# Seven-product form of the up-projection: ScalarE's copy of the first product's first half goes ahead of the last three activations of the pair done last

## The chip, the cores and the metric

One core of a Trainium2 chip runs the whole kernel. The metric is device time in microseconds (us), the median of several executions. The five engines that the text names work in parallel, each through its own queue in order: PE (TensorE), DVE (VectorE), ACT (ScalarE), POOL (GpSimd) and SP (SyncE, which here only issues DMAs). ACT issues DMAs too, from the same queue as its arithmetic.

## The reference

A decoder block over 1024 tokens of width 1024 in float32: two token mixers, then a gated feed-forward part with a causal convolution of width 3. The change lies in the feed-forward part alone:

```
def conv_ffn(h, w_up, conv_w, conv_b, w_down):
    u = h @ w_up                                   # 1024 x 5632
    up = jnp.pad(u, ((0, 0), (CONV_WIDTH - 1, 0), (0, 0)))
    u = sum(up[:, i:i + T] * conv_w[i] for i in range(CONV_WIDTH)) + conv_b
    gate, val = jnp.split(u, 2, axis=-1)           # 22 tiles of 128 columns each
    return (jax.nn.gelu(gate, approximate=True) * val) @ w_down
```

## The kernel before, in words

Every float32 operand is split into a high part (`w_hi`, cast on ACT) and a low part (`w_lo`, a subtraction on POOL or DVE), and a product is three matmuls per block of 128 rows: high by high, high by low, low by high (helper `mm3`, lines 224 to 226).

The up-projection goes over 22 pairs of column tiles (one gate tile j, one value tile j + 22), for two halves of the tokens (`hf` 0 and 1, 512 each). Pairs 3 to 21 (`n` = 0 to 18 in the loop) use a seven-product form: sums and differences of weight blocks and of token blocks replace the eight half products by seven, each of 12 matmuls into one PSUM bank. In the order of the code they are: pX from `w1` (first half), pZ from `w2`, pT from `w2`, pY from `w3`, pX again (second half, added to the same bank), pZ from `w3`, pT from `w4`. The text calls them X1, Z1, T1, Y, X2, Z2 and T2. For the first four pairs (`n` under `NEAR`) X1 and X2 were made earlier and come from DRAM, so the rest speaks of `n` = 4 to 18.

Between the products stand steps that empty the banks: ACT copies X1 to `s1` (line 1188) and Z1 to `s5` (line 1193); DVE adds T1 to `s5` (line 1195) and Y to `s1` (line 1197); ACT copies X2 to `ub` (line 1200); POOL adds `s1` and `s5` (line 1201); DVE adds Z2 and T2 to `s1` (lines 1203 and 1205). X2 is added to the bank that the copy at line 1188 reads, so it waits for that copy; T2 is added to the bank that line 1195 reads.

Then come, for two halves by two tiles, the convolution (`conv`: an activation on ACT at line 1065, two DVE operations at 1066 and 1068) and the gate (`gate`: a Gelu on ACT at 1073, a DVE product at 1074, and the DMA of the result to DRAM, `f_d`, issued from ACT at 1075).

The weights of the next pairs are prepared beside this: SP loads them to `st1` and `st2`, DVE forms `sa` (lines 1168 and 1169), `st2` (1171) and `st1` (1172), ACT casts each and POOL or DVE subtracts (`cut`, lines 1164 and 1165). `sa` has one buffer only: DVE may write the `sa` of the next pair when POOL's subtraction from the present one is over.

The order of each queue is set by the scheduler of the kernel's language, which takes what is ready in a modelled time line, with the order of the code and given priorities behind it: the preparation of weights has `high_priority(offset=WPRIO)`. After the last pair the down-projection follows: it loads `f_d` again (`f_st`, cast to `f_hl` at line 1241, subtraction at 1242) and its weights (lines 212 and 218).

Of the kernel before, what the change touches and what calls it, by code (L numbers as in the profile page):

```python
# [12 lines left out]
AF = mybir.ActivationFunctionType  # L13
# [15 lines left out]
E05 = math.exp(-0.5)  # L29
TWO_PI = 2.0 * math.pi  # L30
WPRIO = 500
MAGIC = 12582912.0
C1 = 6.25
C2 = 0.033203125
# [124 lines left out]
def body(tc, nc, xT, xN, pos, wch, wbrw, wbret, wout, wup, wdn, w2a2, gw2, rows, vecs, consts0, consts1, out):  # L159
    V, S, G, PE = nc.vector, nc.scalar, nc.gpsimd, nc.tensor  # L160
    ctx = ExitStack()

    @contextmanager
    def tile_pool(**kw):
        with tc.tile_pool(**kw) as pool:
            yield Lines(pool)

    with ctx:
# [14 lines left out]
        def C(name):  # L183
            t, o, n = COFF[name]
            return cst[t][:, o:o + n]

        def VC(name):
            o, n = VOFF[name]
            return vct[:, o:o + n]
# [5 lines left out]
        def bank(name, tag="A"):  # L195
            return psB.tile([128, 512], F32, tag=tag, name=name, bufs=BANKS[tag])
# [5 lines left out]
        def load_w(src, kt, full=None, hi=None, lo=None, st=None, eng=None):  # L202

            wp, nb = wpools[cnt[0] % len(wpools)]
            with tc.high_priority(offset=WPRIO if cnt[0] > 3 else 0):
                if st is None:
                    st = wp.tile([128, full or kt, 128], F32, tag="ws", name="w_st", bufs=nb[0])[:, 0:kt, :]
                nc.sync.dma_start(st, src)
            with tc.high_priority(offset=WPRIO if cnt[0] > 1 else 0):
                if hi is None:  # L210
# [64 lines left out]
        with tile_pool(name="x0", bufs=2, reuse_waits="tile") as xp:  # L275
# [22 lines left out]
            for q in range(NJ):  # L298
                xn = xp.tile([128, D], F32, tag="xn", name="xn", bufs=3)
                nc.sync.dma_start(xn, xN[128 * q:128 * q + 128, :])  # L300
                S.activation(xn, xn, AF.Square, accum_out=rsm[:, q:q + 1])
            with tc.high_priority(offset=WPRIO):
                V.tensor_scalar(rsm[:, 8:16], rsm[:, 0:8], 1.0 / D, RMS_EPS, ALU.mult, ALU.add)
# [10 lines left out]
        def proj(w, ps, hf, ts=slice(0, 512)):  # L314
            hi, lo = w
            mm3(ps[:, ts], [(hi[:, k, :], lo[:, k, :], hn[k][hf][0][:, ts], hn[k][hf][1][:, ts]) for k in range(KT)])
# [11 lines left out]
        with pctx, tile_pool(name="p1", bufs=1, reuse_waits="tile", side="right") as p1:  # L328
# [160 lines left out]
            V.tensor_scalar(n, ang, 1.0 / TWO_PI, C("turn"), ALU.mult, ALU.add)  # L489
            V.tensor_scalar(n, n, MAGIC, MAGIC, ALU.add, ALU.subtract)  # L490
            for c_ in (C1, C2, C3):
# [14 lines left out]
        def qk_pair(m):  # L506

            ws = [load_w(wch[14 + 2 * m + e], 8) for e in range(2)]
            for hf in range(2):
                h_ = slice(hf * 512, (hf + 1) * 512)  # L510
                ab = []
                for e in range(2):
                    ps = psA.tile([128, 512], F32, tag="a", name="ps_side")
                    proj(ws[e], ps, hf)
                    with tc.high_priority(offset=WPRIO):
                        t = gp.tile([128, 512], F32, tag=f"qk{e}", name="qk", bufs=1)
# [17 lines left out]
        def side_tile(i):  # L534

            w = load_w(wch[i], 8)
            for hf in range(2):
                ps = psA.tile([128, 512], F32, tag="a", name="ps_side")
                proj(w, ps, hf)
                with tc.high_priority(offset=WPRIO):  # L540
                    ot = gp.tile([128, 512], F32, tag="ot", name="ot")
# [237 lines left out]
        def first_stage(j):  # L779

            nonlocal R
            tk = slice(j * 128, (j + 1) * 128)
            with tc.high_priority(offset=WPRIO):
                zvg = t2.tile([128, 24, 128], F32, name="zvg")
# [272 lines left out]
        def mmb(ps, w, ks, B, first, last):  # L1057
            mm3(ps, [(w[0][:, k, :], w[1][:, k, :], B[n][0], B[n][1]) for n, k in enumerate(ks)],
                first=first, last=last, skip=not first)

        def conv(pool, ub, b, j, src):

            i = j + FT * b
            u = pool.tile([128, 512], F32, tag=f"u{b}", name="u_f")
            S.activation(u, src, AF.Identity, bias=VC("cb")[:, i:i + 1], scale=VC("cw2")[:, i:i + 1])  # L1065
            V.scalar_tensor_tensor(out=u, in0=ub[:, 1:513], scalar=VC("cw1")[:, i:i + 1], in1=u,  # L1066
                                   op0=ALU.mult, op1=ALU.add)
            V.scalar_tensor_tensor(out=u, in0=ub[:, 0:512], scalar=VC("cw0")[:, i:i + 1], in1=u,  # L1068
                                   op0=ALU.mult, op1=ALU.add)
            return u  # L1070

        def gate(j, hf, u0, u1):
            S.activation(u0, u0, AF.Gelu_apprx_tanh)
            V.tensor_tensor(out=u0, in0=u0, in1=u1, op=ALU.mult)
            nc.scalar.dma_start(f_d[hf, j], u0)

# [66 lines left out]
        fp = fctx.enter_context(tile_pool(name="fp", bufs=2, reuse_waits="tile"))  # L1143
        W8 = [128, 8, 128]
        lh, rh_ = slice(0, 4), slice(4, 8)

        for n, j in enumerate(range(NSTD, FT)):
            with tc.high_priority(offset=WPRIO):
                st1 = wp.tile(W8, F32, tag="ws", name="w_st", bufs=2)
                nc.sync.dma_start(st1, wup[j])  # L1150

                st2 = wx.tile(W8, F32, tag="ws", name="w_st", bufs=2) if n else w3s.tile(W8, F32, tag="ws", name="w_st")
                nc.sync.dma_start(st2, wup[j + FT])
                sa = wx.tile(W8, F32, tag="sa", name="w_sa") if n else w3s.tile(W8, F32, tag="wh", name="w_sa")
                if n >= NEAR:
                    w1 = wp.tile(W8, F32R, tag="wh", name="w_hi", bufs=3), wx.tile(W8, F32R, tag="wl", name="w_lo", bufs=3)
                wh = (wx, 2) if n else (wp, 3)
                w2 = (wh[0].tile(W8, F32R, tag="wh", name="w_hi", bufs=wh[1]),
                      wx.tile(W8, F32R, tag="wl", name="w_lo", bufs=3) if n else w3s.tile(W8, F32R, tag="wl", name="w_lo"))
                w3 = wp.tile(W8, F32R, tag="wh", name="w_hi", bufs=3), wp.tile(W8, F32R, tag="wl", name="w_lo", bufs=2)  # L1160
                w4 = wh[0].tile(W8, F32R, tag="wh", name="w_hi", bufs=wh[1]), wp.tile(W8, F32R, tag="wl", name="w_lo", bufs=2)

                def cut(w, ks, src, eng):
                    S.copy(w[0][:, ks, :], src)  # L1164
                    eng.tensor_tensor(out=w[1][:, ks, :], in0=src, in1=w[0][:, ks, :], op=ALU.subtract)  # L1165
                if n >= NEAR:
                    cut(w1, slice(0, 8), st1, G)
                V.tensor_tensor(out=sa[:, lh, :], in0=st2[:, lh, :], in1=st2[:, rh_, :], op=ALU.add)  # L1168
                V.tensor_tensor(out=sa[:, rh_, :], in0=st1[:, lh, :], in1=st2[:, lh, :], op=ALU.subtract)  # L1169
                cut(w2, slice(0, 8), sa, G)  # L1170
                V.tensor_tensor(out=st2[:, lh, :], in0=sa[:, lh, :], in1=st1[:, lh, :], op=ALU.subtract)
                V.tensor_tensor(out=st1[:, rh_, :], in0=st1[:, rh_, :], in1=st2[:, lh, :], op=ALU.subtract)
                cut(w3, lh, st2[:, lh, :], G)
                cut(w3, rh_, st1[:, rh_, :], G)
                cut(w4, lh, st2[:, rh_, :], V)
            if n >= NEAR:
                pX = psA.tile([128, 512], F32, tag="a", name="ps_x")
            pZ = bank("ps_z", "B")
            pT = bank("ps_t", "CY"[n % 2])
            pY = bank("ps_y", "AI"[n % 2])  # L1180
            ub = [fp.tile([128, 1026], F32, tag=f"ub{b}", name="ub") for b in range(2)]
            for b in range(2):
                G.memset(ub[b][:, 0:2], 0.0)
            s1 = fp.tile([128, 512], F32, name="s1")
            s5 = fp.tile([128, 512], F32, name="s5")
            if n >= NEAR:
                mmb(pX, w1, range(4), hn2[0][0:4], True, True)
                S.copy(s1, pX)
            else:
                nc.sync.dma_start(s1, e_d[n, 0])  # L1190
                nc.sync.dma_start(ub[0][:, 2:514], e_d[n, 1])
            mmb(pZ, w2, range(4), T1, True, True)
            S.copy(s5, pZ)
            mmb(pT, w2, range(4, 8), T3, True, True)
            V.tensor_tensor(out=s5, in0=pT, in1=s5, op=ALU.add)
            mmb(pY, w3, range(4), T2, True, True)
            V.tensor_tensor(out=s1, in0=pY, in1=s1, op=ALU.add)
            if n >= NEAR:
                mmb(pX, w1, range(4, 8), hn2[0][4:8], False, True)
                S.copy(ub[0][:, 2:514], pX)  # L1200
            G.tensor_tensor(out=ub[1][:, 514:1026], in0=s1, in1=s5, op=ALU.add)
            mmb(pZ, w3, range(4, 8), hn2[1][4:8], False, True)
            V.tensor_tensor(out=ub[0][:, 514:1026], in0=pZ, in1=s1, op=ALU.add)  # L1203
            mmb(pT, w4, range(4), T4, False, True)
            V.tensor_tensor(out=ub[1][:, 2:514], in0=pT, in1=s1, op=ALU.add)
            for hf in range(2):
                cv = [conv(fp, ub[b][:, 512 * hf:512 * hf + 514], b, j, ub[b][:, 512 * hf + 2:512 * hf + 514])
                      for b in range(2)]
                gate(j, hf, *cv)
        fctx.close()  # L1210
        w3ctx.close()

# [103 lines left out]
```

## Time and profile before

| what | us |
|---|---|
| median of 3 runs (1887.44 to 1890.42) | 1888.04 |
| the profiled execution, its own time | 1895.04 |
| its span, first to last instruction | 1893.2 |
| PE busy in the span | 1786.2 |
| DVE busy | 1182.6 |
| ACT busy | 649.9 |
| POOL busy | 687.0 |

The profiled execution is 7.00 us longer than the median of the runs. PE is busy in 94% of the span, but a busy PE is not PE at its peak, since the ends of matmuls are modelled; what counts is where PE stands still, and behind whom. The seven-product pairs with X1 and X2 (`n` = 4 to 18) fill about 1300 to 1618 us of the span.

### The profile page before, as it was taken

What the parts mean: (1) busy time and instruction counts of PE and PEld (TensorE: products, weight loads), DVE (VectorE), ACT (ScalarE), POOL (GpSimd) and SP (SyncE); (2) the same over time, 40 slices, a digit from 0 to 9 for tenths busy, and PEclk for the clock granted to TensorE, in tenths of its full rate; (3) what the DMA queues carried; (4) which work ended last, traced back from release to release, by engine and by line L of the source; (5) the groups of instructions that cost most, each with busy time, mean ns of one, the idle gap of its engine ahead of it and who ended that gap; (6) DMA issues with size and microseconds to landing.
All of it is one profiled execution on the core that took longest, in us unless ns stands there. A gap on an engine that the chain in (4) does not pass through costs nothing.

```text
span 1893.2 us, 27391 instructions
## 1 busy us (share of the span) xinstructions
PE 1786.2 (94%) x10610; PEld 1448.0 (76%) x10610; DVE 1182.6 (62%) x2068; ACT 649.9 (34%) x993; POOL 687.0 (36%) x491
## 2 busy tenths in 40 slices
PE   8779999999999999999999999888999999989996
PEld 7667778788777788888788778676777777868885
DVE  4786584755666634663444837789888887753413
ACT  6543211111111113322343435544434444443320
POOL 1344523311122122111463744554554454222523
PEclk9989999999999999999999999999999999999998
DMA  8233532433423225555653835433222222665531
GB/s 287 86 114 100 186 86 70 134 90 89 115 88 115 72 84 159 176 178 167 205 167 102 261 116 168 167 117 99 85 78 72 86 69 88 218 205 144 188 92 45
DMA packets 202690, 244.44 MB, mean 129 GB/s; under 512 B 60992, under 2 KB 136256, under 8 KB 201536
## 3 DMA queue, kind: packets, MB, share of 16 engines
q1 hardware_dynamic: 125712, 171.11, 29.8%
q10 hardware_dynamic: 76848, 71.59, 11.6%
q8 instruction: 83, 1.36, 0.3%
q14 instruction: 47, 0.39, 0.1%
HBM read 177.10 MB, written 65.54 MB: 128 GB/s over the span
## 4 chain that ended last, share of the span: by engine, by line
PE 53%; DVE 18%; DMA 8%; issue 4%; POOL 3%; ACT 3%; ACTq 0%; SPq 0%; DVEq 0%; POOLq 0%
PE ps_side L225 7%; PE ps_side L224 7%; PE ps_side L226 7%; DVE u_f L1066 4%; PE ps_dn L226 3%; PE ps_dn L225 3%; PE ps_dn L224 3%; DMA w_st<-in_wup_dram 2%; DVE u_f L1068 2%; POOL w_lo L1165 2%; DVE w_sa L1169 2%; PE ps_o L225 1%; PE ps_o L226 1%; PE ps_o L224 1%; DVE w_sa L1168 1%
## 5 line engine op out<-in xcount | busy, mean ns | idle before, releaser
L218 POOL TENSOR_TENSOR w_lo<-w_st,w_hi 128x1024 fp32r<-128x1024 f32 (+2 forms) x111 | 259.8, 2341 | 515.7 <-ACT w_hi L212 183.5
L212 ACT CAST w_hi<-w_st 128x1024 fp32r<-128x1024 f32 (+2 forms) x162 | 161.7, 999 | 412.6 <-PE ps_side L225 130.7
L225 PE MATMUL ps_side<-hnl,w_hi 128*128 128x512 f32 x640 | 256.2, 400 | 0.0
L224 PE MATMUL ps_side<-hnh,w_hi 128*128 128x512 f32 x640 | 255.6, 399 | 0.0
L226 PE MATMUL ps_side<-hnh,w_lo 128*128 128x512 f32 x640 | 254.9, 398 | 0.0
L224 PEld LDWEIGHTS ps_side<-hnh,w_hi 128*128 128x128 f32 x640 | 121.0, 189 | 26.9 <-issue 1.5
L225 PEld LDWEIGHTS ps_side<-hnl,w_hi 128*128 128x128 f32 x640 | 121.0, 189 | 26.5 <-issue 1.5
L226 PEld LDWEIGHTS ps_side<-hnh,w_lo 128*128 128x128 f32 x640 | 121.1, 189 | 26.3 <-issue 0.8
L218 DVE TENSOR_TENSOR w_lo<-w_st,w_hi 128x1024 fp32r<-128x1024 f32 (+1 forms) x51 | 65.2, 1279 | 82.3 <-ACT w_hi L212 40.6
L1066 DVE SCALAR_TENSOR_TENSOR u_f<-ub,vct,u_f 128x512 f32<-128x512 f32 x88 | 102.1, 1164 | 13.2 <-ACT u_f L1065 11.5
L1165 POOL TENSOR_TENSOR w_lo<-w_st,w_hi 128x512 fp32r<-128x512 f32 (+1 forms) x53 | 105.5, 2012 | 3.8 <-ACT w_hi L1164 2.3
L1065 ACT ACTIVATE u_f<-ub,vct 128x512 f32<-128x512 f32 x76 | 59.8, 812 | 124.4 <-DVE ub L1203 99.2
L224 PE MATMUL ps_rw<-hnh,w_hi 128*128 128x512 f32 (+1 forms) x224 | 87.7, 392 | 13.1 <-ACT hnh L289 6.8
L225 PE MATMUL ps_rw<-hnl,w_hi 128*128 128x512 f32 (+1 forms) x224 | 86.7, 387 | 0.5 <-DVE hnl L290 0.5
L226 PE MATMUL ps_rw<-hnh,w_lo 128*128 128x512 f32 (+1 forms) x208 | 80.0, 385 | 0.0
L226 PE MATMUL ps_b<-y_hi,w_lo 128*128 128x512 f32 x192 | 75.2, 392 | 2.8 <-DVE w_lo L218 1.8
L1068 DVE SCALAR_TENSOR_TENSOR u_f<-ub,vct,u_f 128x512 f32<-128x512 f32 x88 | 76.9, 892 | 0.2
L224 PE MATMUL ps_b<-y_hi,w_hi 128*128 128x512 f32 x192 | 75.2, 392 | 0.7 <-ACT w_hi L212 0.6
L225 PE MATMUL ps_b<-y_lo,w_hi 128*128 128x512 f32 x192 | 74.9, 390 | 0.0
L224 PE MATMUL ps_dn<-f_k,w_hi 128*128 128x512 f32 (+1 forms) x198 | 72.4, 366 | 0.0
L226 PE MATMUL ps_dn<-f_k,w_lo 128*128 128x512 f32 (+1 forms) x198 | 72.4, 366 | 0.0
L225 PE MATMUL ps_dn<-f_k,w_hi 128*128 128x512 f32 (+1 forms) x198 | 72.2, 366 | 0.0
(418 smaller groups left out, 4346.6 us busy)
## 6 DMA issues: line engine op xcount, KB each, us to landing
w_st<-in_wup_dram SPq DMA_DIRECT2D x54, 512.0 KB, 3.5
w_st<-in_wch_dram SPq DMA_DIRECT2D x52, 512.0 KB, 3.9
w_st<-in_wdn_dram SPq DMA_DIRECT2D x38, 512.0 KB, 4.0
pj_d<-ot ACTq DMA_DIRECT2D x64, 256.0 KB, 2.2
zvg<-pj_d SPq DMA_DIRECT2D x8, 1536.0 KB, 8.9
f_d<-u_f ACTq DMA_DIRECT2D x44, 256.0 KB, 2.1
L<-L_d SPq DMA_DIRECT2D x8, 1344.0 KB, 5.9
w_st<-in_wbret_dram SPq DMA_DIRECT2D x16, 512.0 KB, 3.9
```

The source lines that it names most:

```text
L212: S.copy(hi, st)
L218: eng.tensor_tensor(out=lo, in0=st, in1=hi, op=ALU.subtract)
L224: PE.matmul(ps, wh, xh, start=first and a == 0, stop=False, skip_group_check=skip)
L225: PE.matmul(ps, wh, xl, start=False, stop=False, skip_group_check=skip)
L226: PE.matmul(ps, wl, xh, start=False, stop=last and a == n - 1, skip_group_check=skip)
L1065: S.activation(u, src, AF.Identity, bias=VC("cb")[:, i:i + 1], scale=VC("cw2")[:, i:i + 1])
L1066: V.scalar_tensor_tensor(out=u, in0=ub[:, 1:513], scalar=VC("cw1")[:, i:i + 1], in1=u, op0=ALU.mult, op1=ALU.add)
L1068: V.scalar_tensor_tensor(out=u, in0=ub[:, 0:512], scalar=VC("cw0")[:, i:i + 1], in1=u, op0=ALU.mult, op1=ALU.add)
L1165: eng.tensor_tensor(out=w[1][:, ks, :], in0=src, in1=w[0][:, ks, :], op=ALU.subtract)
L1168: V.tensor_tensor(out=sa[:, lh, :], in0=st2[:, lh, :], in1=st2[:, rh_, :], op=ALU.add)
L1169: V.tensor_tensor(out=sa[:, rh_, :], in0=st1[:, lh, :], in1=st2[:, lh, :], op=ALU.subtract)
```

## The change

The last part of a pair's work (the two value halves' convolution, the second Gelu, the gate products and their DMAs) is put into a function `rest`, which the next pair calls just behind its copy of X1, at priority offset `GPRIO` and with an ordering edge: what `rest` puts on ACT's queue stands behind that copy. The gate halves' convolutions and the first Gelu stay where they were.

```
+GPRIO = 40
...
-        def gate(j, hf, u0, u1):
-            S.activation(u0, u0, AF.Gelu_apprx_tanh)
+        def gate(j, hf, u0, u1, gelu=True):
+            if gelu:
+                S.activation(u0, u0, AF.Gelu_apprx_tanh)
...
             if n >= NEAR:
                 mmb(pX, w1, range(4), hn2[0][0:4], True, True)
-                S.copy(s1, pX)
+                c1 = S.copy(s1, pX)
+                with tc.issue_after(c1.ins), tc.high_priority(offset=GPRIO):
+                    rest()
             else:
+                rest()
...
-            for hf in range(2):
-                cv = [conv(fp, ub[b][:, 512 * hf:512 * hf + 514], b, j, ub[b][:, 512 * hf + 2:512 * hf + 514])
-                      for b in range(2)]
-                gate(j, hf, *cv)
+            def part(b, hf, j=j, ub=ub):
+                return conv(fp, ub[b][:, 512 * hf:512 * hf + 514], b, j, ub[b][:, 512 * hf + 2:512 * hf + 514])
+
+            u0 = [part(0, hf) for hf in range(2)]
+            S.activation(u0[0], u0[0], AF.Gelu_apprx_tanh)
+
+            def rest(j=j, part=part, u0=u0):
+                gate(j, 0, u0[0], part(1, 0), gelu=False)
+                gate(j, 1, u0[1], part(1, 1))
+        rest()
```

The queues of PE, POOL and SP keep their order. ACT's and DVE's change at the same places in 14 pairs. ACT's queue before, in a pair in the middle (s1_13051 is the copy of X1; u_f the convolution's result; w_sa the sum of weights that is cast for the next pair; f_d the result in DRAM):

```order
L1164 CAST w_hi_13027<-w_st_13018 128x512
L1065 ACTIVATE u_f_12998<-ub_12897,vct_76 128x512
L1065 ACTIVATE u_f_13009<-ub_12897,vct_76 128x512
L1073 ACTIVATE u_f_13005<-u_f_13005 128x512
L1188 COPY s1_13051<-ps_x_13043 128x512
L1193 COPY s5_13052<-ps_z_13044 128x512
L1075 DMA f_d_10242<-u_f_12994 128x512
L1075 DMA f_d_10242<-u_f_13005 128x512
L1164 CAST w_hi_13174<-w_sa_13171 128x1024
```

ACT's queue now, the same place (s1_13038 is the copy; lines are those of the changed file, up to 17 higher):

```order
L1169 CAST w_hi_13014<-w_st_13005 128x512
L1195 COPY s1_13038<-ps_x_13030 128x512
L1066 ACTIVATE u_f_13053<-ub_12884,vct_76 128x512
L1066 ACTIVATE u_f_13059<-ub_12884,vct_76 128x512
L1075 ACTIVATE u_f_12998<-u_f_12998 128x512
L1203 COPY s5_13039<-ps_z_13031 128x512
L1077 DMA f_d_10242<-u_f_12994 128x512
L1169 CAST w_hi_13161<-w_sa_13158 128x1024
L1077 DMA f_d_10242<-u_f_12998 128x512
```

The copy has gone ahead of three activations, and, besides, the cast of w_sa has gone ahead of the second DMA to f_d. This second exchange stands in 13 of the 14 pairs; in the last it is the cast of an f_hl that goes ahead of the DMA.

On DVE one operation of the convolution changes places with the difference at line 1172; before and now, in another pair:

```order
L1165 TENSOR_TENSOR w_lo_12877<-w_st_12867,w_hi_12876 128x512
L1066 SCALAR_TENSOR_TENSOR u_f_12847<-ub_12746,vct_76,u_f_12847 128x512
L1172 TENSOR_TENSOR w_st_13016<-w_st_13016,w_st_13018 128x512
L1066 SCALAR_TENSOR_TENSOR u_f_12858<-ub_12746,vct_76,u_f_12858 128x512
L1068 SCALAR_TENSOR_TENSOR u_f_12847<-ub_12746,vct_76,u_f_12847 128x512
```

and on DVE now:

```order
L1170 TENSOR_TENSOR w_lo_12864<-w_st_12854,w_hi_12863 128x512
L1177 TENSOR_TENSOR w_st_13003<-w_st_13003,w_st_13005 128x512
L1067 SCALAR_TENSOR_TENSOR u_f_12902<-ub_12733,vct_76,u_f_12902 128x512
L1067 SCALAR_TENSOR_TENSOR u_f_12908<-ub_12733,vct_76,u_f_12908 128x512
L1069 SCALAR_TENSOR_TENSOR u_f_12902<-ub_12733,vct_76,u_f_12902 128x512
```

The difference of weights comes one place sooner and the value half's first operation one place later; all else stays. In the last pair, where the down-projection's work mixes in, an f_hl cast on ACT goes ahead of the activations too, and its subtraction on DVE ahead of four convolution operations. ACT's queue there before:

```order
L1164 CAST w_hi_13631<-w_st_13622 128x512
L1065 ACTIVATE u_f_13602<-ub_13501,vct_76 128x512
L1065 ACTIVATE u_f_13613<-ub_13501,vct_76 128x512
L1073 ACTIVATE u_f_13609<-u_f_13609 128x512
L1241 CAST f_hl_13797<-f_st_13795 128x512
L1188 COPY s1_13655<-ps_x_13647 128x512
```

There the cast stood last but one. ACT's queue at the same place now (s1_13642 is the copy):

```order
L1169 CAST w_hi_13618<-w_st_13609 128x512
L1258 CAST f_hl_13797<-f_st_13795 128x512
L1195 COPY s1_13642<-ps_x_13634 128x512
L1066 ACTIVATE u_f_13657<-ub_13488,vct_76 128x512
L1066 ACTIVATE u_f_13663<-ub_13488,vct_76 128x512
L1075 ACTIVATE u_f_13602<-u_f_13602 128x512
```

Here the copy stands behind a cast that waits for a load from DRAM, as it did before, and both stand ahead of the activations.

## Rows read from the trace of the kernel before

**Rows 1.** Waits by engine, 1340 to 1590 us: total us, times, longest

```profile
ACT w_hi L1164 <- DVE u_f L1074: 37.4, 12, 3.3
DVE w_sa L1168 <- POOL w_lo L1165: 33.6, 12, 2.9
...
PE ps_x L224 <- ACT s L1188: 15.3, 13, 1.3
```

**Rows 2.** Timeline of PE, 1440 to 1465: start, duration, [idle before, releaser]

```profile
1444.58 0.39 PE L226 MATMUL ps_y<-b_hi,w_lo 128*128 128x512 f32 x1
1446.13 0.50 PE L224 MATMUL ps_x<-b_hi,w_hi 128*128 128x512 f32 x1 [1.16 <-ACT s L1188]
...
1451.72 0.39 PE L224 MATMUL ps_t<-b_hi,w_hi 128*128 128x512 f32 x1
...
1454.44 0.39 PE L224 MATMUL ps_x<-b_hi,w_hi 128*128 128x512 f32 x1
```

**Rows 3.** Timeline of ACT, 1440 to 1465

```profile
1442.57 0.61 ACT L1164 CAST w_hi<-w_st 128x512 fp32r<-128x512 f32 x1
1443.57 1.52 ACT L1065 ACTIVATE u_f<-ub,vct 128x512 f32<-128x512 f32 x2 [0.39 <-DVE ub L1205]
1444.99 0.61 ACT L1073 ACTIVATE u_f<-u_f 128x512 f32<-128x512 f32 x1
1445.51 0.56 ACT L1188 COPY s<-ps_x 128x512 f32<-128x512 f32 x1
1445.98 0.58 ACT L1193 COPY s<-ps_z 128x512 f32<-128x512 f32 x1
1448.68 0.93 ACTq L1075 DMA_DIRECT2D f_d<-u_f  x2
1449.65 1.05 ACT L1164 CAST w_hi<-w_sa 128x1024 fp32r<-128x1024 f32 x1 [3.09 <-DVE u_f L1074]
```

**Rows 4.** Timeline of DVE, 1440 to 1465

```profile
1442.85 0.68 DVE L1205 TENSOR_TENSOR ub<-ps_t,s 128x512 f32<-128x512 f32 x1
...
1447.96 1.29 DVE L1074 TENSOR_TENSOR u_f<-u_f 128x512 f32<-128x512 f32 x2
1449.16 0.69 DVE L1195 TENSOR_TENSOR s<-ps_t,s 128x512 f32<-128x512 f32 x1
1449.76 0.68 DVE L1197 TENSOR_TENSOR s<-ps_y,s 128x512 f32<-128x512 f32 x1
1453.21 1.77 DVE L1168 TENSOR_TENSOR w_sa<-w_st 128x512 f32<-128x512 f32 x1 [2.77 <-POOL w_lo L1165]
```

**Rows 5.** Timeline of POOL, 1440 to 1465

```profile
1450.78 2.40 POOL L1165 TENSOR_TENSOR w_lo<-w_sa,w_hi 128x1024 fp32r<-128x1024 f32 x1 [2.52 <-ACT w_hi L1164]
1453.14 1.29 POOL L1201 TENSOR_TENSOR ub<-s,s 128x512 f32<-128x512 f32 x1
```

**Rows 6.** Chain that ended last: start, us, what

```profile
1350.58 1.77 DVE w_sa L1168
...
1449.28 0.33 ACTq L1075
...
1576.39 1.77 DVE w_sa L1168
```

**Rows 7.** Timeline, 1326 to 1337: a POOL pass beside DVE

```profile
1327.35 2.62 POOL L1165 TENSOR_TENSOR w_lo<-w_sa,w_hi 128x1024 fp32r<-128x1024 f32 x1
...
1327.63 0.69 DVE L1195 TENSOR_TENSOR s<-ps_t,s 128x512 f32<-128x512 f32 x1
...
1328.23 2.29 DVE L1074 TENSOR_TENSOR u_f<-u_f 128x512 f32<-128x512 f32 x1
```

**Rows 8.** Timeline of ACT, 1585 to 1640, the last pair

```profile
1608.61 0.60 ACT L1241 CAST f_hl<-f_st 128x512 fp32r<-128x512 f32 x1
...
1614.08 0.62 ACT L1241 CAST f_hl<-f_st 128x512 fp32r<-128x512 f32 x1 [3.91 <-DMA f_st<-f_d]
```

**Rows 9.** Waits of PE, 1590 to 1700

```profile
PE ps_dn L226 <- DVE w_lo L218: 5.8, 4, 2.8
```

More of the change, by code (lines that the diff above doesn't have):

```diff
@@ L1145, in body, with rest @@
         lh, rh_ = slice(0, 4), slice(4, 8)
+        def rest():
+            pass
         for n, j in enumerate(range(NSTD, FT)):
```

## Prediction

> **What bounds the kernel now.** I read the page's slices first, then the waits of the stretch of regular pairs, the chain that ended last, and the timelines of PE, ACT, DVE and POOL in one pair. In the waits the reader sees one entry for PE that matters: the second half of the first product (X2) waits for ACT's copy of the first half, 13 times in this window [rows 1]. On PE's timeline, Y's last matmul starts at 1444.58 and X2's first at 1446.13 [rows 2]; undisturbed matmuls follow each other by a twelfth of a product, and a product takes 2.72 us (1451.72 to 1454.44, [rows 2]), so 0.23 us. X2 could have started at 1444.81 and is 1.32 us late. ACT's timeline says why: the copy at 1445.51 stands behind two activations and a Gelu that start at 1443.57 and 1444.99 [rows 3], though X1, which it reads, was done long before: the next pair's X1 starts at 1454.44 [rows 2], so this pair's, one period of 20.53 us (below) earlier, at 1433.9, and it was over at 1436.6.
>
> But PE's wait isn't what sets the period. The chain passes line 1168 at 1350.58 and at 1576.39 [rows 6], 11 periods later: (1576.39 - 1350.58) / 11 = 20.53 us a pair. PE needs 7 x 2.72 = 19.04. In the chain between there is no PE. It goes round like this: DVE's two gate products (1447.96, 1.29 us, [rows 4]), ACT's two DMA issues of their results (from 1448.68, [rows 3]; the second at 1449.28, [rows 6]), ACT's cast of `sa` (1449.65, after 3.09 us of idling, [rows 3]), POOL's subtraction from it (1450.78, after 2.52 us of idling, [rows 5]), DVE's next write of the one `sa` buffer (1453.21, after 2.77 us of idling, [rows 4]), and through DVE's queue back to the gate products. Three engines stand idle in turn there, each released by the one before: 37.4 us for ACT and 33.6 us for DVE in 12 pairs [rows 1]. PE runs beside this ring and loses in each pair what the ring is longer.
>
> **The copy, moved ahead.** It would follow the cast at 1442.57, 0.61 us long [rows 3]. ACT idles 0.39 us there before the two activations, which wait for DVE's line 1205 (1442.85 + 0.68 = 1443.53, [rows 4]). The copy occupies ACT for 0.47 us (1445.51 to the next start, 1445.98, [rows 3]). Starting about 1443.1, it ends its turn about 1443.57, when the activations started anyway: hidden, or 0.1 us late at the most. DVE takes their first result one place later than before, so that 0.1 is covered too. The price of the move is nothing; were that idle time gone, it would be 0.47 us a pair.
>
> What it gives: X2 no longer waits and PE gains 1.32 us once. It then meets the next wait on the same ring. T2 must not start before DVE's line 1195 has read its bank, at 1449.16 + 0.69 = 1449.85 [rows 4]. With X2 at 1444.81, T2 comes 2 x 2.72 us later, at 1450.25: 0.40 us to spare. In the next pairs PE gains again and waits at T2 instead of X2. So alone this move is worth 1.32 + 0.40 = 1.7 us once, not once per pair.
>
> **The cast of `sa`, moved ahead of the second DMA issue.** This is a side effect of the new order, and it is on the ring. The cast follows the last issue's start by 1449.65 - 1449.28 = 0.37 us. Behind the first issue, at 1448.68, it starts at 1449.05: 0.60 us sooner. Its data and buffer are ready then: `sa` was written in DVE's pass before the gate products, and the bank of weights it overwrites belonged to T1, which PE left before Y, done by 1444.8. POOL's subtraction, DVE's write of `sa`, and all behind them come 0.60 us sooner, and the next pair starts that much sooner: a period of 19.93 us, still above PE's 19.04. The second DMA issue now comes while the cast runs; its landing frees a buffer that is written again only in the next pair's convolution, and the down-projection reads the result far later. 13 casts of `sa` are moved so: 13 x 0.60 = 7.8 us.
>
> Bounds of this term: below, what POOL's pass costs if it overlaps DVE. A pass beside DVE took 2.62 us [rows 7], one by itself 2.40 [rows 5]: 0.22 us, so 0.38 us a pair, 4.9 in all. Above, all that the ring is longer than PE: 20.53 - 19.04 = 1.49 us a pair, 13 x 1.49 = 19.4. I take 0.60, since the nearest rows give it directly, and DVE's lines 1195 and 1197, which POOL's earlier pass would meet, ran at their full speed beside such a pass (0.69 us, [rows 7]).
>
> **DVE's exchange** of a weights difference with a convolution operation: same operations, same sum, no POOL pass beside either (POOL is idle from the end of its previous passes to 1450.78 but for two small fills, [rows 5] shows 2.52 us of idling at its end). Nothing; at most 0.1 us either way.
>
> **The end of the stretch.** In the last pair a cast of `f_hl` (1608.61) comes ahead of the activations, and its subtraction goes ahead of four DVE operations of about 0.7 us. The load of the next `f_st` waits for that subtraction, and ACT later idled 3.91 us for such a load [rows 8]. So between 0 and 4 x 0.7 = 2.8 us sooner. PE's lead of 1.7 us arrives here as well. But the down-projection's start is itself held by its weights (5.8 us of PE waits, [rows 9]), which come by the same DVE, ACT and DMA queues: PE's lead is mostly waited away. Of both together, 0 to 4.5 us, I take 0.7, near the lower end because of that row.
>
> **Sum.** 7.8 + 0.7 = 8.5 us from the profiled execution's 1895.04: 1886.5. That execution is 7.0 us above the median of the runs, so the median goes from 1888.04 to 1879.5.
>
> **A rule weighed.** In rows 7 DVE's gate product beside POOL's pass took 2.29 us, line 1195 beside the same pass 0.69. The Trainium skill, "SBUF — State Buffer", section "Who interferes with whom", says that DVE and GpSimd share a port pair as an exclusive lock, and that it is taken by DVE operations with two SBUF inputs, not by those with one. By that rule lines 1195 and 1197 (one input from PSUM) never wait for POOL, and the earlier pass is free; without it the loss of the fourth case below would be open. The trace agrees in that one pass.
>
> **Rivals.**
> 1. *The ring doesn't shorten, PE's wait only moves from X2 to T2.* For it: DVE, ACT and POOL pass the work round with other waits close by, and one that this trace hides behind the first could step in. Against it: each step of the ring shows idle time of over 2.5 us before it, so nothing else is near. What remains is PE's lead: 1888.04 - 1.7 = 1886.3, less than can be told from no change.
> 2. *The ring loosens altogether and PE's work becomes the bound.* For it: DVE's 1.77 us at line 1168 is mostly POOL's 1.29 us beside it [rows 4, 5], and a small shift can let DVE go first; then several alternating passes shorten. Against it: POOL's next pass starts as its previous one ends, ahead of DVE in the same way as now. Time: 1888.04 - 19.4 = 1868.6.
> 3. *Partial:* the ring gives back 0.2 to 0.4 us of each 0.6. That lies inside the forecast's own range below.
> 4. *Slower.* POOL's pass starts before line 1197 and holds it, as it held the gate product in rows 7. It decides if the pass comes 1450.78 - 1449.76 = 1.02 us sooner relative to DVE; I expect 0.60, so 0.42 us are missing. Then: POOL from 1450.18 to 1452.80, line 1197 until 1453.40, POOL's sum of `s1` and `s5`, which needs it, until 1454.69 (1.29 us, [rows 5]), line 1168 until 1455.29. Now it ends at 1453.21 + 1.77 = 1454.98 [rows 4]. That is 0.31 us a pair later, 13 x 0.31 = 4.0: 1892.0.
>
> **How the numbers follow.** Forecast with its partial case 0.68, rival 1 0.19, rival 2 0.08, rival 4 0.05. About 0.2%, 3.8 us, is what a measurement of this kernel can tell from no change. The forecast's own range goes from 1876 (7.8 + 4.5 saved) to 1884 (4.9 less what the end can cost); nearly all of it is faster by over 0.2%, and so is rival 2. Rival 1 is no change; rival 4 is slower. So faster 0.74, same 0.20, slower 0.06. The range reaches down to 1873, more than halfway to rival 2, and up to 1888 to take in rival 1.
>
> **What would show it.** In the changed kernel's chain, line 1168's successor should come every 19.9 us, not 20.5. ACT's idle time before the cast of `sa` should fall from 3.09 to about 2.5 us, with a DMA issue on either side of it. PE's wait for the copy at X2 should be gone, and a wait for line 1195 at T2 of about 0.9 us a pair should stand in its place. A period still at 20.5 with a T2 wait of 1.5 us is rival 1; PE without waits is rival 2; a DVE line 1197 of over 2 us is rival 4. A gain that shows at 1590 us and is gone at 1700 would mean that the down-projection's loads waited it away, and my term for the end is wrong.

## The result and the profile after

The changed kernel takes 1880.38 us (median of 6 runs, 1876.79 to 1884.47), the kernel before 1889.23 us in the runs beside it (1887.40 to 1895.29): a ratio of 0.9945, 95% interval 0.9928 to 0.9962, and 8.85 us less by the medians (by the ratio it would be 10.4, with 7.2 to 13.6 as its interval). The profiled execution took 1881.99 us with a span of 1880.2.

The chain that ended last still goes through DVE's write of `sa`, now line 1173 (start, us, what; to be set beside [rows 6]):

```profile
1349.22 1.76 DVE w_sa L1173
...
1446.22 2.41 POOL w_lo L1170
1448.65 1.77 DVE w_sa L1173
...
1568.00 1.76 DVE w_sa L1173
```

11 pairs lie between the first and the last row: (1568.00 - 1349.22) / 11 = 19.89 us a pair, where the kernel before took 20.53. The same engines follow each other; the way round has become 0.64 us shorter.

The waits of the changed kernel, 1340 to 1590 us, against [rows 1]:

```profile
ACT w_hi L1169 <- DVE u_f L1076: 38.3, 13, 3.0
DVE w_sa L1173 <- POOL w_lo L1170: 26.0, 12, 2.2
...
PEld ps_t L225 <- DVE s L1205: 10.4, 12, 0.9
PE ps_t L225 <- DVE s L1205: 5.4, 12, 0.5
...
PEld ps_x L225 <- ACT s L1195: 2.3, 11, 0.2
```

In this window PE no longer waits for ACT's copy at the second half of the first product; its weight loads (PEld) do for 0.2 us. A wait for DVE's line 1205 has come at the second half of the third. The waits of ACT and DVE for each other's work are still there, only shorter: they are the ring.

One pair of the changed kernel on ACT (against [rows 3]), by the timeline from 1438 us:

```profile
1438.62 0.60 ACT L1169 CAST w_hi<-w_st 128x512 fp32r<-128x512 f32 x1
1439.12 0.57 ACT L1195 COPY s<-ps_x 128x512 f32<-128x512 f32 x1
1439.61 1.52 ACT L1066 ACTIVATE u_f<-ub,vct 128x512 f32<-128x512 f32 x2
1441.04 0.62 ACT L1075 ACTIVATE u_f<-u_f 128x512 f32<-128x512 f32 x1
1441.56 0.56 ACT L1203 COPY s<-ps_z 128x512 f32<-128x512 f32 x1
1444.73 0.33 ACTq L1077 DMA_DIRECT2D f_d<-u_f  x1
1445.09 1.05 ACT L1169 CAST w_hi<-w_sa 128x1024 fp32r<-128x1024 f32 x1 [2.97 <-DVE u_f L1076]
1445.33 0.33 ACTq L1077 DMA_DIRECT2D f_d<-u_f  x1
```

The copy takes the place of the idle 0.39 us ahead of the activations, which are not late: 1439.61 - 1438.62 = 0.99 us behind the cast's start, 1.00 before. The cast of `sa` now lies between the two DMA issues, 0.36 us behind the first one's start.

The same pair on DVE (against [rows 4]):

```profile
1444.01 1.29 DVE L1076 TENSOR_TENSOR u_f<-u_f 128x512 f32<-128x512 f32 x2
1445.21 0.69 DVE L1205 TENSOR_TENSOR s<-ps_t,s 128x512 f32<-128x512 f32 x1
1445.81 0.68 DVE L1207 TENSOR_TENSOR s<-ps_y,s 128x512 f32<-128x512 f32 x1
1448.65 1.77 DVE L1173 TENSOR_TENSOR w_sa<-w_st 128x512 f32<-128x512 f32 x1 [2.15 <-POOL w_lo L1170]
```

Line 1173 starts 1448.65 - 1444.01 = 4.64 us behind the gate products' start, and 1453.21 - 1447.96 = 5.25 before: 0.61 us less. POOL, by its timeline (against [rows 5]), brings it that far:

```profile
1446.22 2.40 POOL L1170 TENSOR_TENSOR w_lo<-w_sa,w_hi 128x1024 fp32r<-128x1024 f32 x1 [1.91 <-ACT w_hi L1169]
```

In the last pair PE does wait for the copy at X2: there the copy stands behind the cast of `f_hl`, which starts only after 1.43 us of idling (ACT, then PE):

```profile
1598.80 0.62 ACT L1258 CAST f_hl<-f_st 128x512 fp32r<-128x512 f32 x1 [1.43 <-issue]
1599.33 0.58 ACT L1195 COPY s<-ps_x 128x512 f32<-128x512 f32 x1
```

```profile
1599.96 0.50 PE L225 MATMUL ps_x<-b_hi,w_hi 128*128 128x512 f32 x1 [0.89 <-ACT s L1195]
```

### The profile page after: what moved, and what is told of

The parts are those of the page before. It is cut to its first block, busy times and chain, and to the rows that moved or that the text cites. A ratio compares the mean times of both kernels' runs of the same rounds, so it can differ in the third digit from the quotient of the medians.

```text
span 1880.2 us, 27392 instructions
## 1 busy us (share of the span) xinstructions
PE 1788.0 (95%) x10610; PEld 1448.4 (77%) x10610; DVE 1182.3 (63%) x2068; ACT 648.3 (34%) x993; POOL 686.6 (37%) x491
## 4 chain that ended last, share of the span: by engine, by line
PE 56%; DVE 18%; DMA 5%; issue 4%; POOL 3%; ACT 3%; ACTq 0%; SPq 0%; DVEq 0%; POOLq 0%
PE ps_side L226 7%; PE ps_side L225 7%; PE ps_side L227 7%; DVE u_f L1067 4%; PE ps_dn L227 4%; PE ps_dn L226 4%; PE ps_dn L225 4%; DVE u_f L1069 2%; POOL w_lo L1170 2%; PE ps_o L226 1%; PE ps_o L227 1%; PE ps_o L225 1%; DVE w_sa L1174 1%; DVE w_sa L1173 1%; PE ps_b L227 1%
```

## The experiments

All were timed in 5 rounds beside the kernel before; e1 to e4 on one chip, e6 and e7 on another. A period that covers the whole stretch is read from one row of ACT's grouped timeline, 1290 to 1650 us (start of the first and the last of the 15 casts of `sa`; 14 pairs lie between). It is the distance of the casts; where PE's own work becomes the bound, the distance of PE's products has to be read beside it (e3, e6). The three kernels in which it decides most, before, e2 and e1:

```profile
L1164 ACT CAST w_hi<-w_sa x15: 1039/1052/1059, 1306.0 to 1593.3; 128x1024 fp32r<-128x1024 f32 x15
```

```profile
L1171 ACT CAST w_hi<-w_sa x15: 1032/1048/1057, 1300.3 to 1587.9; 128x1024 fp32r<-128x1024 f32 x15
```

```profile
L1166 ACT CAST w_hi<-w_sa x15: 1040/1054/1057, 1307.6 to 1586.7; 128x1024 fp32r<-128x1024 f32 x15
```

That is 287.3 us before, 287.6 in e2 and 279.1 in e1; the changed kernel has 279.0 (1305.3 to 1584.3).

**e1, the cast alone.** The kernel before, and the second DMA issue put behind the cast of `sa`; on no other engine does the order change.

```diff
-            nc.scalar.dma_start(f_d[hf, j], u0)
+            fdma.append(nc.scalar.dma_start(f_d[hf, j], u0))
...
-                    S.copy(w[0][:, ks, :], src)
+                    c = S.copy(w[0][:, ks, :], src)
+                    if src is sa and n > NEAR + 1:
+                        tc.add_manual_dep(fdma[-3].ins, c.ins.name, ...)
```

> The kernel before with one half of the change alone: on ACT the cast of sa goes ahead of the second of the two DMA issues of the gate products, in 13 pairs; the copy of s1 stays behind the activations. Ring theory (the period is set by gate products, DMA issues, cast, POOL's subtraction, DVE's write of sa): the period falls from 20.53 to about 19.9 us, PE goes on waiting for ACT's copy of s1 at ps_x, but less (about 0.6 to 0.9 us a pair in place of 1.2), no wait at ps_t; total 6 to 8 us below the kernel before. Rival (PE's wait for the copy of s1 is what sets the period, and the cast's place is nothing): period 20.5, the wait at ps_x 1.2 as before, total within 1.5 us of the kernel before.

Measured: 1880.07 us against 1889.0, ratio 0.9957, 0.9942 to 0.9971. The period is 279.1 / 14 = 19.94 us. Its waits, 1340 to 1580:

```profile
DVE w_sa L1173 <- POOL w_lo L1170: 26.1, 12, 2.2
...
PEld ps_x L224 <- ACT s L1193: 12.4, 12, 1.7
PE ps_x L224 <- ACT s L1193: 7.3, 12, 1.2
```

PE still waits for the late copy in every pair, 0.6 us by its matmuls and 1.0 by its weight loads, and the kernel has nearly all of the gain. So that wait didn't set the time; the rival falls.

**e2, the copy alone.** The changed kernel with the cast of `sa` held behind both issues.

```diff
+                    if src is sa and n > NEAR + 1:
+                        tc.add_manual_dep(c.ins, fdma[-1].ins.name, ...)
```

> The changed kernel with the other half alone: the copy of s1 ahead of the activations, the cast of sa held behind both DMA issues, as the kernel before has it. Ring theory: period 20.5 us as before; PE's wait leaves ps_x and stands at ps_t for DVE's copy, 1.1 to 1.5 us a pair; total 1 to 3 us below the kernel before (the wait is saved once, at the end of the stretch). Rival (the copy brings the gain by itself): period about 19.9, total 6 to 8 us below.

Measured: 1889.26 us against 1889.0, ratio 1.0011, 0.9998 to 1.0025: no gain. The period is 287.6 / 14 = 20.54 us, as the ring theory has it. The 1 to 3 us that I still expected didn't come in the time (the part on the prediction says where they went). Its waits, 1340 to 1580, show that the wait didn't wander wholly to `ps_t` either:

```profile
PEld ps_t L225 <- DVE s L1210: 9.7, 11, 0.9
PEld ps_x L225 <- ACT s L1200: 9.6, 11, 1.5
PE ps_t L225 <- DVE s L1210: 5.0, 11, 0.5
PE ps_x L225 <- ACT s L1200: 4.9, 11, 1.1
```

On its ACT timeline the two issues together show what the second one costs the cast:

```profile
1442.77 0.93 ACTq L1079 DMA_DIRECT2D f_d<-u_f  x2
1443.74 1.05 ACT L1171 CAST w_hi<-w_sa 128x1024 fp32r<-128x1024 f32 x1 [3.57 <-PE ps_z L227]
```

The cast starts 0.97 us behind the first issue, in the changed kernel 0.36: 0.61 us a pair.

**e3, the cast ahead of both issues.** The changed kernel, with the cast waiting for no gate product. Besides, near the end of the stretch one cast of `f_hl` goes ahead of the copy of X2, where the kernel before has it too.

```diff
+                    if src is sa and n > NEAR + 1:
+                        for d in fdma[-2:]:
+                            tc.add_manual_dep(d.ins, c.ins.name, ...)
```

> The changed kernel with the cast of sa ahead of both DMA issues, so that it waits for no gate product any more. Ring theory: the product leaves the ring; ACT's wait ahead of the cast (35.3 us in 12 pairs of the changed kernel) goes, POOL's pass starts some 3 us earlier, and lies beside a gate product, which then takes 2.3 in place of 1.3 us; DVE's wait for POOL ahead of its write of sa (26.0 in 12) mostly goes; period between 19.04, the products of PE alone, and 19.5, total 5 to 11 us below the changed kernel. Rival (the ring is closed elsewhere, or DVE's lost microsecond a pair takes its place): period 19.8 or more, total within 2 us of the changed kernel or above it.

Measured: 1865.04 us (1864.51 to 1867.36) against 1889.0, ratio 0.9885, 0.9865 to 0.9905. It beats both kernels, the changed one by 15 us by the medians and by 11 by the ratios (0.9885 against 0.9945), where 5 to 11 were expected. PE's busy time in the 240 us from 1340 to 1580 (us, then busy time of PE, PEld, DVE, ACT and POOL with counts, PEclk, DMA share, GB/s), first of the changed kernel and then of e3:

```profile
1340.00:1580.00 240.00, 235.09 (x1019) 189.32 (x1018) 210.84 (x232) 110.62 (x172) 120.76 (x85) 1.00 0.24 79
```

```profile
1340.00:1580.00 240.00, 240.00 (x1060) 198.83 (x1059) 218.10 (x240) 115.86 (x178) 139.86 (x90) 1.00 0.26 86
```

With the ring opened at the gate products, PE doesn't wait at all in this window. The first matmul of the product Y, in pair `n` = 5 and in the last one:

```profile
1335.45 0.39 PE L225 MATMUL ps_y<-b_hi,w_hi 128*128 128x512 f32 x1
...
1582.97 0.39 PE L225 MATMUL ps_y<-b_hi,w_hi 128*128 128x512 f32 x1
```

That is (1582.97 - 1335.45) / 13 = 19.04 us a pair, and each of the 13 distances is 19.04: this is PE's own work, 7 x 2.72. The casts come every (1565.3 - 1302.2) / 14 = 18.79 us, so here they aren't PE's period; they start 4.2 us behind Y (1339.68 in the pair of 1335.45) and at the end 1.4 us behind it (1565.35, 1563.93). On DVE's and POOL's timelines one thing came otherwise than expected:

```profile
1454.38 1.28 DVE L1078 TENSOR_TENSOR u_f<-u_f 128x512 f32<-128x512 f32 x2
...
1457.96 1.77 DVE L1179 TENSOR_TENSOR w_sa<-w_st 128x512 f32<-128x512 f32 x1 [1.10 <-POOL w_lo L1176]
```

```profile
1454.69 3.24 POOL L1176 TENSOR_TENSOR w_lo<-w_sa,w_hi 128x1024 fp32r<-128x1024 f32 x1
```

The two gate products kept their 1.28 us; it was POOL's pass, come second, that took 3.24 in place of 2.40. DVE's wait for POOL fell by half only, to 13.2 us in 12 pairs, and that no longer matters to PE.

**e4, two buffers for `sa`.** The changed kernel with the buffers in turn; the cast then falls ahead of both issues by itself, and orders on DVE, POOL and PE move too.

```diff
-                sa = wx.tile(W8, F32, tag="sa", name="w_sa") if n else ...
+                sa = (wx if n % 2 else fp).tile(W8, F32, tag="sa", name="w_sa", bufs=1) if n else ...
...
-            s5 = fp.tile([128, 512], F32, name="s5")
+            s5 = fp.tile([128, 512], F32, name="s5", bufs=1)
```

> The changed kernel with two buffers for sa, used in turn (the copy s5 gives up its second buffer for the space), so that DVE's write of sa no longer waits for POOL's reading of the one before; with it the order on ACT becomes that of the cast ahead of both DMA issues, and some rows on DVE, POOL and PE move. Ring theory: with the ring cut open, DVE's wait for POOL (26.0 us in 12 pairs) goes, and the period falls to what PE's seven products take, 19.04 to 19.2 us, PE without waits at ps_x and ps_t; total 9 to 12 us below the changed kernel. Rival (PE waits for something else that comes late anyway, the single s5 among them): period 19.6 or more.

Measured: 1886.36 us against 1889.0, ratio 0.9990, 0.9974 to 1.0006. The expectation failed. DVE's wait for POOL is gone, as it had to be, but the period is (1590.8 - 1305.4) / 14 = 20.39 us. DVE's timeline:

```profile
1466.67 0.69 DVE L1173 TENSOR_TENSOR w_sa<-w_st 128x512 f32<-128x512 f32 x1 [1.77 <-DMA w_st<-in_wup_dram]
...
1471.01 2.27 DVE L1076 TENSOR_TENSOR u_f<-u_f 128x512 f32<-128x512 f32 x1
```

The write of `sa` now stands in DVE's queue ahead of the last convolution steps and the gate products, and waits there for its weights; one gate product then runs beside POOL's pass and takes 2.27 us. So this run tells that a buffer which lets the order move can cost what it frees. It doesn't tell which of the moved operations costs how much, nor whether the second buffer alone, at the old order, would open the ring; that wasn't run.

**e6, the cast ahead of both issues, the copy where it was before.**

```diff
-                        tc.add_manual_dep(fdma[-3].ins, c.ins.name, ...)
+                        for d in fdma[-4:-2]:
+                            tc.add_manual_dep(d.ins, c.ins.name, ...)
```

> The kernel before with the cast of sa ahead of both DMA issues, and the copy of s1 left where the kernel before has it, behind the three activations. The changed kernel with the same cast order takes 18.82 us a pair, 1865.0 us in all, with no wait of PE. Theory A (the place of the copy is worth something only where the ring does not bind): PE's weight load goes on waiting for the copy at ps_x, 0.5 to 1.1 us a pair, the period is 19.3 to 19.9 and the total 6 to 16 us above 1865. Theory B (the copy is worth next to nothing either way; its wait was slack of the ring): period 18.8 to 18.9 without a wait at ps_x, total within 2 us of 1865.

Measured: 1867.36 us (1864.87 to 1870.57) against 1889.94, ratio 0.9884, 0.9871 to 0.9898; e3, with the copy moved, has 0.9885. The row of casts:

```profile
L1166 ACT CAST w_hi<-w_sa x15: 1030/1055/1057, 1297.4 to 1560.7; 128x1024 fp32r<-128x1024 f32 x15
```

The casts come every 263.3 / 14 = 18.81 us; PE's Y comes every 19.04 us from 1351.26 to 1579.74, as in e3, and from 1340 to 1580 PE has no wait, with ACT's copy behind the activations as it was. Theory A falls: the wait at `ps_x` that came with every pair was slack of the ring. Just before, PE waits for the copy one more time, where e3 has no wait:

```profile
1334.81 0.50 PE L224 MATMUL ps_x<-b_hi,w_hi 128*128 128x512 f32 x1 [1.24 <-ACT s L1194]
```

That pair takes 20.58 us in e6 and 19.04 in e3: what the copy's place is worth here is 1.54 us once. The times can't tell it: e6's median is 2.4 us above 1865, theory B had allowed 2, but the two ran on different chips and their ratios are equal.

**e7, the changed kernel again.**

> The changed kernel once more, on the same chip as the other run of this call, so that the worth of the copy's place can be read beside the run that moves only the cast. If the copy is worth the 1.7 us of the prediction, the ratio to the kernel before stays near 0.9945 where the run with the cast alone had 0.9957; if it is worth nothing, the two agree, 0.995 to 0.997. The chain of DVE's writes of sa at 19.9 us a pair again.

Measured: 1879.74 us against 1889.94, ratio 0.9949, 0.9936 to 0.9962; the casts go from 1303.1 to 1582.2, 19.94 us a pair. The ratio lies between e1's and the first one of the changed kernel, and all three intervals overlap: whatever the copy adds to the cast is under what these times can tell.

## Why the prediction came out right, and which terms didn't

- *The ring, not PE's wait, sets the period.* Right, and shown: e1 leaves PE's wait in and has the gain, e2 takes the cast's place back and has none, e3 opens the ring and PE's waits are gone. The forecast period was 19.93 us; the chain has 19.89.
- *The cast ahead of the second issue, 0.60 us x 13 = 7.8.* Right: 0.61 us by e2's rows, and by its ratio e1 gains 0.0043 x 1889 = 8.1 us (5.5 to 11.0), by the medians 8.9. In the trace the 15 casts span 287.3 - 279.1 = 8.2 us less.
- *DVE's exchange, nothing.* It fits: e1 has DVE's old order and the gain, e2 has the new order and none.
- *The sign in ACT's idle time.* The idle time before the cast fell to 2.97 us, not to 2.5. The copy of `s5` ends ACT's work 0.48 us sooner too, since the copy of `s1` is no longer ahead of it; e2 has 3.57 us, and 3.57 - 0.60 = 2.97. I took the idle time for a measure of the ring; it also counts what ends before it. The distance from gate products to line 1173 measures the ring alone.
- *The copy, 1.7 us once.* Right in the traces, up to the last pair. From the Y of `n` = 5 to that of the last pair PE takes 257.57 us in the changed kernel (1338.62 to 1596.19) and 259.31 in e1 (1340.94 to 1600.25): 1.7 us for the copy. Without the cast's move it is 1.3 (e2 265.55, before 266.88), with the ring open 1.5 (e3 247.52, e6 249.06). But in the last pair the late copy costs 0.89 us in the changed kernel and 1.50 in e2, where e1 has no wait. From the last cast to the first `ps_dn` matmul the trace has 24.7 us before (1593.3 to 1618.0), 24.8 in e1, 24.0 in the changed kernel and in e2: about 0.8 us of the lead is left at that point, and e2's time shows nothing of it. The prediction had the lead mostly waited away too, but by the down-projection's weights; it is lost before the down-projection starts. The cost of the move was nothing, as forecast.
- *A wait of 0.9 us at T2 in place of X2.* Right by the weight loads, 10.4 / 12 = 0.87 us, and by PE's own delay, 19.89 - 19.04 = 0.85; the matmul rows show half of it.
- *The end of the stretch, 0 to 4.5, taken 0.7.* Smaller than the times can tell: by the medians e1 gains 8.9 us and the changed kernel 8.85, by the ratios 8.1 and 10.4, each with about 3 us either way. The trace's 0.8 is of the forecast size. The gain is not waited away behind the stretch. The two profiled spans even differ by 13.0 us: 9.8 at the first `ps_dn` matmul (1618.04 and 1608.27), the rest in the down-projection. The medians don't have that rest (the profiled execution of before was a long one, 1895.04 us), and I didn't follow it.
- *PE's floor, 7 x 2.72 = 19.04 us.* Right to the hundredth in e3 and e6, and with it the size of rival 2, the ring loose altogether: from the Y of `n` = 5 to that of the last pair e3 takes 266.88 - 247.52 = 19.4 us less than before, as the prediction had it. e3's 1865 us is 3.6 below the 1868.6 given for that rival; what makes up this rest outside the stretch wasn't followed.
- *Rival 4.* POOL's pass starts at 1446.22, line 1207 at 1445.81 with 0.68 us: not held. The rival didn't come about.

So the total, 8.5 us forecast and 8.85 measured, is right by its mechanism and mainly by its one large term. That the two agree to 0.35 us is in part luck, since the measurement itself leaves 7.2 to 13.6. The copy, which the change is about, has 0.8 us of it in the trace and nothing that the times can tell.

## What to carry to other kernels

A wait on the busiest engine can be slack of a ring that runs through the others: divide the chain's distance by the pairs, compare it with that engine's own work, and look where the ring closes. Read that engine's own work from its own rows: what another engine does once a pair can run ahead of it for many pairs (18.8 against 19.04 us in e3). A DMA issue in an arithmetic engine's queue holds what is queued behind it until its data is there; an instruction that doesn't need that data belongs ahead of it (here 0.61 us a pair for the second issue, and 20.53 - 19.04 = 1.5 for both together with the products they wait for, until PE's own work is the bound). When a change does two things, run each alone: the one with the visible wait was worth nothing that the times could tell.

## What the hardware showed that I had not expected

PE's idle time understates what PE loses at a wait, and the waits of its weight loads overstate it. In us a pair, the distance of the first matmuls of Y (mean of 11 pairs, from about 1358 to 1580 us) beside the waits from 1340 to 1580:

| kernel | pair by Y | above 19.04 | idle by matmul rows | waits of weight loads |
|---|---|---|---|---|
| before | 20.53 | 1.49 | 1.18 | 1.60 |
| changed | 19.88 | 0.84 | 0.45 | 1.07 |
| e1 | 19.90 | 0.86 | 0.61 | 1.03 |
| e2 | 20.55 | 1.51 | 0.90 | 1.75 |

The rows of one wait in the changed kernel tell why the idle time is too low:

```profile
1445.08 0.39 PE L227 MATMUL ps_z<-b_hi,w_lo 128*128 128x512 f32 x1
1445.95 0.50 PE L225 MATMUL ps_t<-b_hi,w_hi 128*128 128x512 f32 x1 [0.48 <-DVE s L1205]
```

Undisturbed matmuls start 0.23 us apart though each row is 0.39 long. So this one could have started at 1445.31 and is 0.64 us late, while the idle time counts from the end of the row before, 1445.47.

Who comes first decides between DVE and POOL. In [rows 7] POOL's pass was first, and the gate product took 2.29 us; in e3 the products were first, kept their 1.28 us for the two, and the pass took 0.84 us longer. The Trainium skill, "SBUF — State Buffer", section "Who interferes with whom", says that the order of issue and not the kind of operation decides which of the two is blocked; both traces agree.
